# Normalised input for the last two products, and sums of squares by token without additions ahead of them

## The chip, the cores and the metric

The kernel runs on one core of a Trainium2 chip. The metric is the device time of one execution, in microseconds (us). The time before is given as the median of three runs; a further execution was taken with the hardware profiler, and all rows come from that one.

## The reference, cut to what matters

The kernel computes one block: a norm, a state-space mixer and a dilated attention side by side, an FFN with a causal convolution, a gated projection of a side input `p`, and a last norm. Only the end of it concerns the change:

```
h  = h + (gelu(gate) * (u2 @ ffn_w_up)) @ ffn_w_down
u3 = rms_norm(h, ple_norm_g)
h  = h + sigmoid(u3 @ ple_w_gate) * (p @ ple_w_proj)
return rms_norm(h, final_norm_g)
```

`x` is 512 tokens by 1024 features, all float32. `rms_norm(x, g)` is `x * rsqrt(mean(x*x) + 1e-6) * g`, with the mean over the features of a token.

## The kernel before, in words

**Layout.** Features lie on the 128 partitions and tokens along the free axis, so `h` is 8 tiles of 128 features by 512 tokens. A product `W.T @ u` for 128 output features runs over 8 blocks k of input features and leaves a 128x512 tile in PSUM.

**Three matmuls for one.** Each operand is split into a high part (rounded to the chip's fast float32 form, `F32R`) and a low part (the rest). `mm3` (lines 148 to 151) issues high by high, high by low and low by high. A weight chunk of 128x1024, the weights of one output tile, is loaded by DMA into `wr`, copied to `wh` by ScalarE (line 128) and subtracted to `wl` by VectorE (line 129); each has three buffers in turn. `u_split` (lines 158 to 160) makes the two parts of an input: the gain g of the norm is in there as a scale, the norm's factor by token is not.

**The factor comes in behind the product.** A factor by token can be taken out of the product, so the kernel computes `(h*g) @ W` first and multiplies the PSUM tile by `rb3` (the factor, spread over all partitions) afterwards. `rstd_full` (lines 235 to 253) makes `rb3` from the sum of squares `acc3`, beside the first products of this stage.

**The last stage (lines 998 to 1095).** The input `u3` has been split while the FFN's last products ran, and `pp` holds `p @ ple_w_proj`. The loop of lines 1031 to 1038 makes output tiles m = 0 to 5 over all 512 tokens: `gemm` into `eps`, then `ple(m)` (lines 1012 to 1025): VectorE multiplies PSUM by `rb3` (line 1014), ScalarE takes `tanh` (line 1023), two VectorE instructions (`stt`, recorded at line 422) fold in `pp` and update `h`. `sq_acc` squares the new `h` on ScalarE (line 204) and adds it to `acc4` on VectorE (line 205); `scale_g` (line 1028) writes `hg`, the new `h` times the last gain.

The tiles m = 6 and 7 are made twice, for two groups of 256 tokens (`LAST`, lines 1058 to 1080): m = 6 and 7 of the first group, then m = 6 and 7 of the second. The text calls these four products 6a, 7a, 6b and 7b; instructions of theirs have 256 columns. Their `ple` is the same but that in 7b the `tanh` (line 1017) writes a tile of its own and is followed by a tiny square root (line 1019), which makes the engine load the table for the square root early. The squares of 6a, 7a and 6b are added to `acc4` (line 1075); that of 7b is not.

**Sums and output.** `finish` (lines 1045 to 1055) sums over the features on TensorE: `stats` (lines 1006 to 1010) takes 128 tokens of a tile of squares as weights and a column of ones as the moving operand, one matmul for 128 tokens, run by the chip in two passes. For the first group one `stats` call on `acc4` is enough; it is put inside product 7b (`STATS_AT`, with an offset of -15 in the order). For the second group `stats` is called on `acc4` and on the squares of 7b. From the sums comes the last norm's factor by token, `y4`: with VectorE alone for the first group (`rstd_dve`), with a square root on ScalarE for the second (`rstd_of`). Then TensorE transposes `hg` to tokens on partitions (tile `fT`, line 1087), 4 transposes a tile, 8 tiles; ScalarE (line 1091) or VectorE (recorded at line 417) scales each by `y4` into `fo`, as the letters of `EVAC` say (A or D), and SyncE issues the store of 256 KB (line 1094).

**What sets the order.** Tiles of the pools have fixed numbers of buffers: 5 for `mm_tile` (PSUM, the products and half of the transposes), 4 for `t_tile` (the working tiles of `ple`, the squares). When the program is built, every engine gets its instructions in one fixed order, chosen by priority (the order of the program, moved ahead by `ahead(n)`: 300 for weights, `TAIL` = 40 for the end) among those that the builder's own clock thinks ready. On the chip each engine keeps that order, and an instruction that must wait holds up all behind it.

```
def mm3(ps, st, mv, first, last):
    PE.matmul(ps, st[0], mv[0], start=first, stop=False)
    PE.matmul(ps, st[0], mv[1], start=False, stop=False)
    PE.matmul(ps, st[1], mv[0], start=False, stop=last)
```

Of the kernel before, what the change touches and what calls it, by code (L numbers as in the profile page):

```python
# [10 lines left out]
F32R = mybir.dt.float32r  # L11
I32 = mybir.dt.int32
AF = mybir.ActivationFunctionType
ALU = mybir.AluOpType
# [5 lines left out]
KD = D // P  # L20
SEQ = 512
# [8 lines left out]
V_MIX, V_GB, V_GLUB, V_FFN, V_CW, V_CB, V_PLE, V_FIN, V_N = 0, 8, 24, 28, 36, 102, 124, 132, 140  # L30
# [9 lines left out]
WARM = 8  # L40
TAIL = 40
ST_AHEAD = -15
EVAC = "ADADADAD"
STATS_AT = (7, 0)
NLAST = 2
LAST = ((0, 1), (2, 3))
# [18 lines left out]
def tile_hybrid_block(ctx: ExitStack, tc: tile.TileContext, xT, xtok, pT, W, vecs, consts, ssm, out):  # L65
    nc = tc.nc
    ACT, DVE, POOL, PE = nc.scalar, nc.vector, nc.gpsimd, nc.tensor
# [8 lines left out]
    def slot(i, shape, name, dt=F32):  # L76
        return sb.tile([P] + shape, dt, tag=f"s{i}", name=name)
# [4 lines left out]
    def mm_tile(name):  # L82
        return pm.tile([P, 512], F32, tag="mm", name=name)

    def ax_tile(name):
        return px.tile([P, 512], F32, tag="ax", name=name)

    def t_tile(name):
        return ring.tile([P, 512], F32, tag="t", name=name, bufs=4)
# [12 lines left out]
    def v1(col):  # L102
        return vec[:, col:col + 1]
# [5 lines left out]
    def ahead(offset=AHEAD):  # L109
        return tc.high_priority(offset=offset)  # L110
# [37 lines left out]
# [5 lines that stand above are left out]
    def u_tiles(name):  # L153
        uh = [slot(f"uh{j}", [4, SEQ], f"{name}h{j}", F32R) for j in range(2)]
        ul = [slot(f"ul{j}", [4, SEQ], f"{name}l{j}", F32R) for j in range(2)]
        return ([uh[k // 4][:, k % 4, :] for k in range(KD)], [ul[k // 4][:, k % 4, :] for k in range(KD)])
# [42 lines left out]
    def sq_acc(acc, k, src):  # L199
        if k == 0:  # L200
            ACT.activation(acc, src, AF.Square)
        else:
            t = t_tile("sq")
            ACT.activation(t, src, AF.Square)
            DVE.tensor_tensor(acc, acc, t, op=ALU.add)
# [29 lines left out]
    def rstd_full(acc, name):  # L235
        hi = ring.tile([P, SEQ], F32R, tag="t", name=name + "_hi", bufs=4)
        lo = ring.tile([P, SEQ], F32R, tag="t", name=name + "_lo", bufs=4)
        ACT.activation(hi, acc, AF.Copy)
        DVE.tensor_tensor(lo, acc, hi.bitcast(F32), op=ALU.subtract)
        ps = ax_tile(name + "_ps")  # L240
        PE.matmul(ps, ones_r, hi, start=True, stop=False)
        PE.matmul(ps, ones_r, lo, start=False, stop=True)
        m = t_tile(name + "_m")
        DVE.tensor_scalar(m, ps, 1.0 / D, EPS, op0=ALU.mult, op1=ALU.add)
        t = t_tile(name + "_t")
        ACT.activation(t, m, AF.Sqrt)
        y = sb.tile([P, SEQ], F32, tag="acc", name=name + "_y")
        DVE.reciprocal(y, t)
        DVE.tensor_tensor(t, y, y, op=ALU.mult)
        DVE.tensor_tensor(t, t, m, op=ALU.mult)  # L250
        DVE.tensor_scalar(t, t, -0.5, 1.5, op0=ALU.mult, op1=ALU.add)
        DVE.tensor_tensor(y, y, t, op=ALU.mult)
        return y
# [151 lines left out]
    def gemm(ps, kt, mv):  # L405
        for k in range(kt):
            mm3(ps, wT.next(), (mv[0][k], mv[1][k]), k == 0, k == kt - 1)
# [4 lines left out]
    def tt(o, a, b, op):  # L412
        DVE.tensor_tensor(o, a, b, op=op)  # L413
# [7 lines left out]
    def stt(o, a, s, b, o0, o1):  # L421
        DVE.scalar_tensor_tensor(o, a, s, b, op0=o0, op1=o1)
# [445 lines left out]
    for m in range(2):  # L868
        ps = mm_tile("v0")
# [8 lines left out]
    for m in range(16):  # L878
        ps = mm_tile("gps")
# [10 lines left out]
    def split(hi, lo, src):  # L890
        ACT.activation(hi, src, AF.Copy)
        tt(lo, src, hi.bitcast(F32), ALU.subtract)
# [11 lines left out]
    for m in range(4):  # L904
        ps = mm_tile("lps")
        gemm(ps, 4, (parts(yh, 4), parts(yl, 4)))
        t = t_tile("lg")
# [8 lines left out]
    h = slot("x", [KD, SEQ], "h")  # L916
# [25 lines left out]
    for m in range(KD):  # L942
        ps = mm_tile("ops")
# [9 lines left out]
    u3 = None  # L953
    for part in range(2):
# [4 lines left out]
        for mi in range(HALF):  # L959
            m = part * HALF + mi  # L960
# [9 lines left out]
            t = t_tile("cv")  # L970
# [9 lines left out]
        if part == 1:  # L980
            u3 = u_tiles("u3")
            acc3 = sb.tile([P, SEQ], F32, tag="acc", name="acc3")
        for m in range(KD):
            ps = mm_tile("dps")
# [13 lines left out]
    for m in range(KD):  # L998
        ps = mm_tile("pps")
        gemm(ps, 2, (parts(ph, 2), parts(pl, 2)))  # L1000
        ACT.activation(pp[m // 4][:, m % 4, :], ps, AF.Copy)
    acc4 = slot("g1", [SEQ], "acc4")
# [3 lines left out]
    def stats(st, src, n, first, last):  # L1006

        for i in range(n):
            PE.matmul(st[:, i:i + 1], src[:, i * 128:(i + 1) * 128], ones[:, 0:1], start=first and i == 0, stop=last,
                      skip_group_check=True)  # L1010

    def ple(m, ps, c, last=False):
        t = t_tile("pg_")[:, c]
        tt(t, ps, rb3[:, c], ALU.mult)
        if last:
            th = t_tile("th")[:, c]
            ACT.activation(th, t, AF.Tanh, scale=0.5)

            ACT.activation(warm, th[:, 0:1], AF.Sqrt, bias=ones[:, 0:1], scale=0.0)
            stt(t, th, 1.0, pp[m // 4][:, m % 4, c], ALU.add, ALU.mult)  # L1020
            stt(h[:, m, c], t, 0.5, h[:, m, c], ALU.mult, ALU.add)
            return
        ACT.activation(t, t, AF.Tanh, scale=0.5)
        stt(t, t, 1.0, pp[m // 4][:, m % 4, c], ALU.add, ALU.mult)
        stt(h[:, m, c], t, 0.5, h[:, m, c], ALU.mult, ALU.add)

    def scale_g(m, c):
        ACT.activation(hg[m // 4][:, m % 4, c], h[:, m, c], AF.Copy, scale=v1(V_FIN + m))

    everything = slice(0, SEQ)  # L1030
    for m in range(KD - NLAST):
        ps = mm_tile("eps")
        gemm(ps, KD, u3)
        if m == 0:
            rb3 = rstd_full(acc3, "n3")
        ple(m, ps, everything)
        sq_acc(acc4, m, h[:, m, :])
        scale_g(m, everything)


    tail = range(KD - NLAST, KD)
    wl_ = [[wT.next() for k in range(KD)] for m in tail]
    y4 = []

    def finish(rs, c, sq, rstd):
        st = ax_tile("st4")
        if sq is None:
            with ahead(ST_AHEAD):
                stats(st, acc4[:, c], len(rs), True, True)
        else:  # L1050
            with ahead(TAIL):
                stats(st, acc4[:, c], len(rs), True, False)
                stats(st, sq, len(rs), False, True)
        with ahead(TAIL):
            y4.append(rstd(st[:, 0:len(rs)], f"n4_{rs[0]}", len(rs)))

    waiting = []
    for gi, rs in enumerate(LAST):
        c = slice(rs[0] * 128, rs[-1] * 128 + 128)
        end = gi == len(LAST) - 1  # L1060
        for m in tail:
            ps = mm_tile("eps")[:, 0:128 * len(rs)]
            for k in range(KD):
                if waiting and (m, k) == STATS_AT:
                    waiting.pop()()
                mm3(ps, wl_[m - tail[0]][k], (u3[0][k][:, c], u3[1][k][:, c]), k == 0, k == KD - 1)
            with ahead(TAIL):
                ple(m, ps, c, end and m == KD - 1)
                sq = t_tile("sq")[:, c]
                if m < KD - 1:  # L1070
                    ACT.activation(sq, h[:, m, c], AF.Square)
                else:
                    tt(sq, h[:, m, c], h[:, m, c], ALU.mult)
                if m < KD - 1 or not end:
                    tt(acc4[:, c], acc4[:, c], sq, ALU.add)
            scale_g(m, c)
        if end:
            finish(rs, c, sq, rstd_of)
        else:
            waiting.append(functools.partial(finish, rs, c, None, rstd_dve))  # L1080
    n = 0
    for rs, y in zip(LAST, y4):
        for j in range(2):
            for r in rs:
# [4 lines left out]
                yr = y[:, r - rs[0]:r - rs[0] + 1]  # L1089
                if EVAC[n] == "A":  # L1090
                    ACT.activation(o, pt, AF.Copy, scale=yr)
# [145 lines left out]
```

## Time and profile before

| | |
|---|---|
| median of 3 runs | 802.42 us (801.52 to 802.46) |
| the profiled execution, its own time | 801.21 us |
| its span (first to last instruction) | 799.4 us |
| busy: TensorE, VectorE, ScalarE | 99%, 62%, 43% of the span |
| the last stage's products (`eps`) | 743.16 to 788.3 us |
| stores of the output | first issued at 791.32 us, last at 795.7 us |

The page gives each engine's busy time and the chain of work that ended last: from the last instruction back, at each step to what released it. PE is TensorE, PEld its weight loads, DVE VectorE, ACT ScalarE, SP SyncE, whose queue issues the DMAs. A row of the timeline gives start, duration, engine, line, operation, the tile written and the tiles read, and in brackets how long the engine had been idle and who released it. Instructions overlap a little, so the step from one start to the next is shorter than a duration.

### The profile page before, as it was taken

The page shows a single profiled execution, that of the slowest core. Times are in us where ns is not written, and L with a number is a line of the kernel's source. Part 1 is how long each engine was busy: PE and PEld are TensorE (multiplying, and loading weights), DVE is VectorE, ACT ScalarE, POOL GpSimd, SP SyncE. Part 2 cuts the span into 40 slices and gives each one's busy share as a digit, 9 for nine tenths or more (in the row PEclk, how much of TensorE's full clock was granted, in tenths as well). Part 3 has the DMA queues.
Part 4 walks back from the last instruction along what each step waited for, and adds up shares of the span by engine and source line. Part 5 has one row for each costly group of instructions (what it writes and reads, how often), then busy time and mean ns, then how long its engine had stood idle before and what let it go on. Part 6 is the DMA issues. An engine that isn't in the chain of part 4 may idle for free.

```text
span 799.4 us, 10889 instructions
## 1 busy us (share of the span) xinstructions
PE 789.4 (99%) x4302; PEld 651.7 (82%) x4302; DVE 494.2 (62%) x960; ACT 346.0 (43%) x551; POOL 10.9 (1%) x10
## 2 busy tenths in 40 slices
PE   9999999999999999999999999999999999999996
PEld 7888888788777788888888888888888888888886
DVE  6974799933556558665865565333565565445586
ACT  6763634344444453344544343122344343335464
POOL 2001000000000000000000000000000000000000
PEclk9999999999999999999999999999999999999998
DMA  7721122231111223623323323323323322322302
GB/s 286 265 90 61 46 84 75 80 106 51 56 55 60 75 81 103 210 84 127 104 81 106 106 80 104 105 83 103 105 81 105 106 84 100 106 85 100 103 4 106
DMA packets 23811, 78.99 MB, mean 99 GB/s; under 512 B 2640, under 2 KB 3024, under 8 KB 23760
## 3 DMA queue, kind: packets, MB, share of 16 engines
q1 hardware_dynamic: 23616, 78.22, 29.0%
q8 instruction: 34, 0.56, 0.3%
q14 instruction: 17, 0.14, 0.1%
q10 hardware_dynamic: 144, 0.07, 0.0%
HBM read 76.18 MB, written 2.10 MB: 98 GB/s over the span
## 4 chain that ended last, share of the span: by engine, by line
PE 83%; DVE 10%; ACT 3%; issue 2%; DMA 1%; SPq 0%; DVEq 0%; ACTq 0%
PE dps L149 5%; PE pu L149 5%; PE pu L150 5%; PE pg L150 5%; PE pg L149 5%; PE dps L151 5%; PE dps L150 5%; PE pg L151 5%; PE pu L151 5%; PE gps L149 4%; PE gps L150 3%; PE gps L151 3%; PE pa L151 2%; PE pa L150 2%; DVE E L413 2%; PE pa L149 2%
## 5 line engine op out<-in xcount | busy, mean ns | idle before, releaser
L128 ACT ACTIVATE wh<-wr 128x1024 fp32r<-128x1024 f32 (+1 forms) x132 | 138.3, 1047 | 295.8 <-issue 66.3
L129 DVE TENSOR_TENSOR wl<-wr,wh 128x1024 fp32r<-128x1024 f32 (+1 forms) x132 | 159.2, 1206 | 69.9 <-ACT wh L128 69.4
L150 PE MATMUL pu<-u2l,wh 128*128 128x512 f32 x176 | 68.5, 389 | 0.0
L149 PE MATMUL pu<-u2h,wh 128*128 128x512 f32 x176 | 68.5, 389 | 0.0
L151 PE MATMUL pg<-u2h,wl 128*128 128x512 f32 x176 | 68.5, 389 | 0.0
L149 PE MATMUL pg<-u2h,wh 128*128 128x512 f32 x176 | 68.5, 389 | 0.0
L150 PE MATMUL pg<-u2l,wh 128*128 128x512 f32 x176 | 68.5, 389 | 0.0
L149 PE MATMUL dps<-ah,wh 128*128 128x512 f32 x176 | 68.5, 389 | 0.0
L150 PE MATMUL dps<-al,wh 128*128 128x512 f32 x176 | 68.5, 389 | 0.0
L151 PE MATMUL dps<-ah,wl 128*128 128x512 f32 x176 | 68.5, 389 | 0.0
L151 PE MATMUL pu<-u2h,wl 128*128 128x512 f32 x176 | 68.5, 389 | 0.0
L149 PE MATMUL pa<-wh,u1h 128*128 128x512 f32 x160 | 63.4, 398 | 0.0
L150 PE MATMUL pa<-wl,u1h 128*128 128x512 f32 x160 | 62.9, 393 | 0.0
L151 PE MATMUL pa<-wh,u1l 128*128 128x512 f32 x160 | 62.6, 393 | 0.1
L149 PE MATMUL gps<-u1h,wh 128*128 128x512 f32 x128 | 51.8, 404 | 0.0
L151 PE MATMUL gps<-u1h,wl 128*128 128x512 f32 x128 | 50.3, 393 | 0.0
L150 PE MATMUL gps<-u1l,wh 128*128 128x512 f32 x128 | 50.3, 393 | 0.0
L413 DVE TENSOR_TENSOR ext<-pg,n_y 128x512 f32<-128x512 f32 x22 | 15.2, 692 | 44.1 <-PE pg L151 44.1
L151 PEld LDWEIGHTS dps<-ah,wl 128*128 128x128 f32 x176 | 33.0, 188 | 6.9
L149 PEld LDWEIGHTS pu<-u2h,wh 128*128 128x128 f32 x176 | 33.0, 188 | 6.9
L151 PEld LDWEIGHTS pu<-u2h,wl 128*128 128x128 f32 x176 | 33.0, 188 | 6.9
L151 PEld LDWEIGHTS pg<-u2h,wl 128*128 128x128 f32 x176 | 33.0, 188 | 6.9
(305 smaller groups left out, 1499.6 us busy)
## 6 DMA issues: line engine op xcount, KB each, us to landing
wr<-in_W_dram SPq DMA_DIRECT2D x128, 512.0 KB, 3.2
xt<-in_xtok_dram SPq DMA_DIRECT2D x4, 512.0 KB, 8.0
h<-in_xT_dram SPq DMA_DIRECT2D x8, 256.0 KB, 4.8
out_dram<-fo SPq DMA_DIRECT2D x8, 256.0 KB, 2.3
x<-in_xT_dram SPq DMA_DIRECT2D x7, 256.0 KB, 5.4
wr<-in_W_dram SPq DMA_DIRECT2D x4, 256.0 KB, 5.3
cst<-in_consts_dram SPq DMA_DIRECT2D x1, 568.0 KB, 10.6
sp<-in_ssm_dram SPq DMA_DIRECT2D x1, 544.0 KB, 6.9
```

The lines of the kernel that those rows point to most:

```text
L128: ACT.activation(hi[:, c], raw[:, c], AF.Copy)
L129: DVE.tensor_tensor(lo[:, c], raw[:, c], hi[:, c].bitcast(F32), op=ALU.subtract)
L149: PE.matmul(ps, st[0], mv[0], start=first, stop=False)
L150: PE.matmul(ps, st[0], mv[1], start=False, stop=False)
L151: PE.matmul(ps, st[1], mv[0], start=False, stop=last)
L413: DVE.tensor_tensor(o, a, b, op=op)
```

## The change

The second group's inputs are made anew, with the norm's factor in them. As soon as `rb3` is there (behind product m = 0), `h * g * rb3` of the last 256 tokens is computed for all 8 feature blocks and split into two tiles `us`, which take the places of `ml` and `praw`. Products 6b and 7b read `us` in place of `u3`, so their PSUM needs no multiplication by `rb3`: `tanh` reads it directly. The squares of 6a, 7a and 6b are no longer added to `acc4`; `finish` gets the list of them and `stats` is called on `acc4` and on each. `EVAC` gives all four tiles of the first group to ScalarE.

```diff
-EVAC = "ADADADAD"
+EVAC = "AAAAADAD"
...
-    def ple(m, ps, c, last=False):
+    def ple(m, ps, c, scaled=False, last=False):
         t = t_tile("pg_")[:, c]
-        tt(t, ps, rb3[:, c], ALU.mult)
+        if not scaled:
+            tt(t, ps, rb3[:, c], ALU.mult)
         if last:
             th = t_tile("th")[:, c]
-            ACT.activation(th, t, AF.Tanh, scale=0.5)
+            ACT.activation(th, ps, AF.Tanh, scale=0.5)
...
-        ACT.activation(t, t, AF.Tanh, scale=0.5)
+        ACT.activation(t, ps if scaled else t, AF.Tanh, scale=0.5)
...
+    cl = slice(LAST[-1][0] * 128, SEQ)
     for m in range(KD - NLAST):
         ps = mm_tile("eps")
         gemm(ps, KD, u3)
         if m == 0:
             rb3 = rstd_full(acc3, "n3")
+
+            us = [slot(n, [KD, cl.stop - cl.start], f"us{j}", F32R) for j, n in enumerate(("qk2", "v"))]
+            for k in range(KD):
+                t = t_tile("us")[:, 0:cl.stop - cl.start]
+                stt(t, h[:, k, cl], v1(V_PLE + k), rb3[:, cl], ALU.mult, ALU.mult)
+                split(us[0][:, k, :], us[1][:, k, :], t)
         ple(m, ps, everything)
...
-    def finish(rs, c, sq, rstd):
+    def finish(rs, c, sqs, rstd, early):
         st = ax_tile("st4")
-        if sq is None:
-            with ahead(ST_AHEAD):
-                stats(st, acc4[:, c], len(rs), True, True)
-        else:
-            with ahead(TAIL):
-                stats(st, acc4[:, c], len(rs), True, False)
-                stats(st, sq, len(rs), False, True)
+        with ahead(ST_AHEAD if early else TAIL):
+            stats(st, acc4[:, c], len(rs), True, False)
+            for i, sq in enumerate(sqs):
+                stats(st, sq, len(rs), False, i == len(sqs) - 1)
...
-                mm3(ps, wl_[m - tail[0]][k], (u3[0][k][:, c], u3[1][k][:, c]), k == 0, k == KD - 1)
+                mv = (us[0][:, k, :], us[1][:, k, :]) if end else (u3[0][k][:, c], u3[1][k][:, c])
+                mm3(ps, wl_[m - tail[0]][k], mv, k == 0, k == KD - 1)
             with ahead(TAIL):
-                ple(m, ps, c, end and m == KD - 1)
-                sq = t_tile("sq")[:, c]
+                ple(m, ps, c, end, end and m == KD - 1)
+                sqs.append(t_tile("sq")[:, c])
                 if m < KD - 1:
-                    ACT.activation(sq, h[:, m, c], AF.Square)
+                    ACT.activation(sqs[-1], h[:, m, c], AF.Square)
                 else:
-                    tt(sq, h[:, m, c], h[:, m, c], ALU.mult)
-                if m < KD - 1 or not end:
-                    tt(acc4[:, c], acc4[:, c], sq, ALU.add)
+                    tt(sqs[-1], h[:, m, c], h[:, m, c], ALU.mult)
```

`split(hi, lo, src)` is a copy on ScalarE (line 891) and a subtraction on VectorE; `stt` and `tt` are one VectorE instruction each.

## Rows read from the trace of the kernel before

**Rows 1.** The page: busy time of each engine.

```profile
PE 789.4 (99%) x4302; PEld 651.7 (82%) x4302; DVE 494.2 (62%) x960; ACT 346.0 (43%) x551; POOL 10.9 (1%) x10
```

**Rows 2.** The chain that ended last, 785 to 799.4: start, us, what.

```profile
788.25 0.34 DVE acc L413
788.66 0.34 DVE pg__6376 L413
789.03 0.42 ACT th L1017
789.47 1.28 ACT L1019
790.76 0.30 ACT warm L1019
791.06 0.40 ACT hg L1028
791.46 1.15 ACT fo L1091 x2
793.61 0.75 DVE fo L417
```

**Rows 3.** Stretches: us, PE, PEld, DVE, ACT, POOL busy (x), clock, DMA share, GB/s.

```profile
758.87:765.00 6.13, 6.13 (x28) 5.07 (x28) 5.71 (x8) 3.35 (x5) 0.00 (x0) 1.00 0.12 48
765.00:772.96 7.96, 7.96 (x36) 6.57 (x35) 5.56 (x8) 5.46 (x8) 0.00 (x0) 1.00 0.01 2
772.96:782.40 9.44, 9.44 (x68) 8.89 (x67) 7.72 (x14) 4.85 (x9) 0.00 (x0) 1.00 0.00 0
```

**Rows 4.** Timeline of VectorE.

```profile
758.87 0.69 DVE L413 TENSOR_TENSOR pg__6011<-eps,n_y 128x512 f32<-128x512 f32 x1
...
785.40 0.43 DVE L413 TENSOR_TENSOR sq<-h 128x256 f32<-128x256 f32 x1
785.74 0.42 DVE L413 TENSOR_TENSOR pg__6323<-eps,n_y 128x256 f32<-128x256 f32 x1
786.07 0.42 DVE L413 TENSOR_TENSOR acc<-acc,sq 128x256 f32<-128x256 f32 x1
...
790.09 0.15 DVE L224 SCALAR_TENSOR_TENSOR n_y<-n_t,n_y 128x2 f32<-128x2 f32 x1
790.21 0.42 DVE L422 SCALAR_TENSOR_TENSOR h<-pg__6376,h 128x256 f32<-128x256 f32 x1
790.55 0.74 DVE L417 TENSOR_SCALAR fo<-fT,n_y 128x512 f32<-128x512 f32 x1
791.21 0.41 DVE L413 TENSOR_TENSOR sq<-h 128x256 f32<-128x256 f32 x1
```

**Rows 5.** Timeline of ScalarE.

```profile
765.28 1.06 ACT L128 ACTIVATE wh<-wr 128x1024 fp32r<-128x1024 f32 x1 [2.32 <-issue]
...
784.05 0.40 ACT L1023 ACTIVATE pg__6289<-pg__6289 128x256 f32<-128x256 f32 x1
```

**Rows 6.** Timeline of TensorE, products 7b and what follows.

```profile
784.77 0.28 PE L149 MATMUL eps<-u3h,wh 128*128 128x256 f32 x1
...
786.57 0.36 PE L1009 MATMUL st<-ones,acc 128*128 128x1 f32 x2
...
788.04 0.28 PE L151 MATMUL eps<-u3h,wl 128*128 128x256 f32 x1
788.16 0.60 PE L1087 MATMUL fT<-cst,hg 128*128 128x128 f32 x4
788.64 0.61 PE L1009 MATMUL st<-ones,acc 128*128 128x1 f32 x4
789.11 2.78 PE L1087 MATMUL fT<-cst,hg 128*128 128x128 f32 x22
```

**Rows 7.** Stretches at the end, columns as in rows 3.

```profile
792.00:792.50 0.50, 0.50 (x6) 0.48 (x6) 0.45 (x2) 0.50 (x2) 0.00 (x0) 1.00 0.61 238
...
795.00:795.50 0.50, 0.00 (x0) 0.00 (x0) 0.02 (x1) 0.00 (x0) 0.00 (x0) 0.72 0.66 246
795.50:796.00 0.50, 0.00 (x0) 0.00 (x0) 0.00 (x0) 0.00 (x0) 0.00 (x0) 0.50 1.03 381
```

**Rows 8.** The queue of SyncE, 788 to 800.

```profile
791.32 4.81 SPq L1094 DMA_DIRECT2D out_dram<-fo  x8
```

More of the change, by code (lines that the diff above doesn't have):

```diff
@@ L1060, in tile_hybrid_block @@
         end = gi == len(LAST) - 1
+        sqs = []
         for m in tail:
@@ L1065, in tile_hybrid_block @@
                     waiting.pop()()
-                mm3(ps, wl_[m - tail[0]][k], (u3[0][k][:, c], u3[1][k][:, c]), k == 0, k == KD - 1)
+                mv = (us[0][:, k, :], us[1][:, k, :]) if end else (u3[0][k][:, c], u3[1][k][:, c])
+                mm3(ps, wl_[m - tail[0]][k], mv, k == 0, k == KD - 1)
             with ahead(TAIL):
-                ple(m, ps, c, end and m == KD - 1)
-                sq = t_tile("sq")[:, c]
+                ple(m, ps, c, end, end and m == KD - 1)
+                sqs.append(t_tile("sq")[:, c])
                 if m < KD - 1:
-                    ACT.activation(sq, h[:, m, c], AF.Square)
+                    ACT.activation(sqs[-1], h[:, m, c], AF.Square)
                 else:
-                    tt(sq, h[:, m, c], h[:, m, c], ALU.mult)
-                if m < KD - 1 or not end:
-                    tt(acc4[:, c], acc4[:, c], sq, ALU.add)
+                    tt(sqs[-1], h[:, m, c], h[:, m, c], ALU.mult)
             scale_g(m, c)
         if end:
-            finish(rs, c, sq, rstd_of)
+            finish(rs, c, sqs, rstd_of, False)
         else:
-            waiting.append(functools.partial(finish, rs, c, None, rstd_dve))
+            waiting.append(functools.partial(finish, rs, c, sqs, rstd_dve, True))
     n = 0
```

## The prediction

> **What bounds the kernel now.** I read the page first: TensorE is busy 99% of the span [rows 1], so elsewhere only what lengthens or shortens TensorE's work counts. The chain of waits says where this stops: it leaves TensorE at about 770 us and runs over VectorE and ScalarE to the end, and through product 7b it runs over the addition of the squares of 6b, the multiplication by `rb3`, `tanh`, the table load, the tiny square root, `hg` and the output's scaling [rows 2]. So 1.3 us of table load and 0.3 us of square root stand on the path, and the change starts just in front of them. Third, the stretches of the last stage [rows 3] show how much room VectorE and ScalarE have for the new work; fourth, the timelines [rows 4 to 6] give prices and queue order; last, the stretches after 792 us [rows 7] show what the stores do. They keep the DMA engines full: the share is 0.61 in the first half microsecond, about 1.0 from then on but for one dip to 0.66 at 795.0, and it ends near 797.9. The span ends at 799.4. So from the first store on it is bandwidth that counts: 8 times 256 KB at some 385 GB/s are 5.45 us, and the dip is worth only 0.17 us.
>
> **The change part by part.** All sums are made against the profiled execution, 801.21 us with a span of 799.4. The four executions shown are 801.21, 801.52, 802.42 and 802.46, their mean 801.9; the profiled one lies 0.7 below that mean and 1.2 below the median.
>
> *The new input `us`.* It adds 8 multiplications, 8 copies and 8 subtractions of 256 columns, placed in the program ahead of `ple(0)`. On VectorE an instruction of this size lasts 0.42 but starts 0.34 after its neighbour (785.40, 785.74, 786.07) [rows 4]: 16 of them are 16 x 0.34 = 5.4 us, or 16 x 0.42 = 6.7 if they don't overlap. From `rb3` at 758.87 to 782.40 VectorE is busy 5.71 + 5.56 + 7.72 = 19.0 of 23.5 us [rows 3], so 4.5 are free, and 0.9 to 2.2 us run over. I take 0.9, since the 16 depend on each other only through ScalarE, and eight feature blocks can overlap. ScalarE gets 8 x 0.40 = 3.2 us [rows 5], against 23.5 - 13.7 = 9.8 free: nothing. TensorE wants `us` only at 781.9, behind 7a; that cover is some 15 us. What moves back is `ple(0)`, from 758.87 to about 766. It frees a PSUM buffer which the sixth product needs at about 770.7, so TensorE doesn't wait while this delay stays under 11 us.
>
> *The squares of the first group.* `sq` of 7a is done at 785.40 + 0.43 = 785.82. With 0.9 of overflow less the addition of 6a's squares (0.34) it is done at about 786.4. TensorE takes the sums at 786.57 [rows 6], so it is just in time.
>
> *The sums themselves.* For the first group there are three sources in place of one: 6 matmuls of two passes in place of 2, that is 8 passes more, and they stand inside 7b. What a pass costs there can be read: 7b takes 788.16 - 784.77 = 3.39 us, and 24 steps of 0.12 are 2.88, so the 4 passes of before cost 0.51, or 0.13 each. Behind the product 4 take 789.11 - 788.64 = 0.47, or 0.12 each [rows 6]. So 8 more cost 1.0 us; they cost nothing on this path if the queue puts them behind 7b. I take 1.0, because the place in the program, inside 7b, is unchanged: the last matmul ends at 789.3 in place of 788.32. The Trainium skill (TensorE: Matmul & The Clock Gate, "Wait — 56ns, not 53.3ns?") says that matmuls of few columns can follow each other every 25 ns or so; 8 passes would be 0.2 us by that and the sum below about 0.8 lower. The trace disagrees with 0.12 to 0.13; each pass here loads 128 columns of new weights, which by the same page's section "LDWEIGHTS (loading the stationary operand)" takes about 107 ns, and this the trace bears out.
>
> *`tanh` reads PSUM.* Before, 7b ended at 788.32, the multiplication started at 788.58 because VectorE was still adding, and `tanh` at 789.03 [rows 2, 4]. Now `tanh` follows TensorE alone: 789.3 and a few hundredths. That is 0.3 to 0.4 later than before, not earlier: the multiplication (0.34 on the chain) and the addition in front (0.34) go, and the passes take more than that back. The table load then ends near 791.1 and the tiny square root near 791.4.
>
> *The squares of 7b.* Before, a scaling of an output tile sat on VectorE ahead of them, 790.55 to 791.21 [rows 4]. It is gone, so they start right behind `h`: at 790.7 in place of 791.2, even with the later `tanh`. The second group's factor is then ready some 0.2 to 0.5 earlier.
>
> *The first group's scaling on ScalarE.* This pays for it. Before, VectorE did the first tile at 790.55, while ScalarE was still in its table load, and the first store went out at 791.32 [rows 4, 8]. Now the first tile must wait for ScalarE: 791.4 if it goes ahead of `hg`, 791.8 if behind it. With 0.62 for a tile (1.24 for two) it is done at 792.0 to 792.4, 0.7 to 1.1 later than before. From there ScalarE gives a tile every 0.62 us and the stores need 0.68, so bandwidth leads again, and the dip (0.17) closes since the second group's tiles come no later than they are wanted. Sum for the end: 0.7 to 1.1 less 0.2 to 0.3 for the dip and an easier start, **+0.6 us**. The end of the queue says +0.35: ScalarE's last tile is done at about 795.6, the last store issued near 796.05 in place of 795.7. I take +0.6, from the larger of the two conditions.
>
> **The rivals.**
>
> *A, the forecast (0.46):* +0.6, on the mean 802.5 us. No change that can be measured: about 0.2%, or 1.6 us, is what a measurement of this kernel can tell from none.
>
> *B, the passes are cheap or fall behind 7b (0.26).* Then `tanh` starts at 788.36, the load ends at 790.1, ScalarE is free at 790.4 and the first group's factor, ready at 790.24 before [rows 4], no longer waits: the first tile is done at 791.1, 0.2 earlier, and the dip closes: -0.4, 801.5 us. For it speaks that the queue's order is made by the builder's clock, which may think 7a's squares later; against it the rows of 0.13. The skill's 25 ns leads here too.
>
> *C, faster (0.10).* VectorE's removed work is all on the path (0.34 + 0.34 in front of `tanh`, 0.66 of the scaling, 0.26 of waiting at 788.32 to 788.58: 1.6) and the stores start as much earlier. That takes the first group's factor by 789, ahead of the table load; -1.7, 800.2 us. Against it: the factor of the first group hangs on 7a's squares, which come no sooner.
>
> *D, slower (0.18).* The place is ScalarE's queue at 763 to 766. There a weight copy waits 2.32 us for TensorE to let go of a buffer [rows 5]. If copies of `us` stand behind it, VectorE's subtractions wait with them, all four `t` buffers are taken, and VectorE stands still with its room used up. It decides from the point where 7a's squares come later than 786.6, of which only 0.2 us is left: from there each microsecond stops TensorE inside 7b by as much. Of the 2.32 about 2.1 at most arrive, 1.6 in the middle: +0.6 + 1.6 = +2.2, 804.1 us. For it speaks that VectorE is full on paper already; against it that the builder sees ScalarE busy too and may put the copies in front.
>
> **How the numbers follow.** A is the likeliest: 802.5 us. A and B are both inside 0.2%, 0.46 + 0.26 = 0.72; C gives 0.10 for faster, D 0.18 for slower. The range runs from 800.8 (between B and C; it leaves C out) to 804.2 (the middle of D; its upper half is left out), so 0.10 and 0.09 lie outside.
>
> **What would show it.** In the changed profile: 16 new VectorE instructions of 256 columns between 759 and 767, no wait of TensorE before 784; 12 passes of `st` inside 7b and its last matmul near 789.3; `tanh` of 7b released by TensorE within 0.1 us; the squares of 7b directly behind `h`; the first store issued at 792.0 to 792.4 and a DMA share of 1.0 without the dip. A first store before 791.2 makes A wrong in favour of B or C; a gap on TensorE in front of `st`, with VectorE idle near 765, makes it D. The forecast fails as well if the stores are not full from the first on.

## The result, and the profile after

The changed kernel takes 807.78 us, the median of 5 runs (807.19 to 808.61), beside 802.46 us for the kernel before in 5 runs (801.52 to 803.00). The ratio is 1.0071, with a 95% interval of 1.0059 to 1.0082: **slower by about 5.7 us** (0.0071 x 802.46; 4.7 to 6.6). The forecast was 802.5, with a range that ended at 804.2.

The profiled execution took 808.02 us, with a span of 806.2, so its span is 6.8 us above that of before. Not all of it is the change's: the last step of `rb3` starts at 759.09 here and at 758.14 before, behind identical code, and in the other profiles below it lies between 758.4 and 759.5. This leaves 6.8 - 0.95 = 5.85 us behind `rb3`.

Busy time of each engine, on the page of the changed kernel (beside [rows 1]):

```profile
PE 792.3 (98%) x4314; PEld 653.3 (81%) x4314; DVE 497.4 (62%) x969; ACT 349.7 (43%) x561; POOL 10.9 (1%) x10
```

VectorE works 3.2 us more than before (497.4 - 494.2). That is little, and its share of the span stays at 62%. A loss of 5.85 us can't be read from this row.

The chain that ended last, from 757 us to the end (start, us, what; compare [rows 2], which shows the end of that of before):

```profile
759.82 1.28 DVE us L422 x3
...
762.56 1.14 DVE wl L129
...
767.58 1.28 ACT L1024
...
779.65 0.70 DVE h L422
780.44 0.63 ACT sq L204
781.07 0.62 ACT hg L1029
781.69 0.53 ACT pg__6203 L1024
...
782.96 0.70 DVE h L422
```

Before, the chain left TensorE at about 770 us. Now it is already off TensorE when `us` starts on VectorE; it runs on over `ple(0)`, the load of the table for `tanh` (767.58) and then tile by tile: `h` on VectorE, squares, `hg` and `tanh` on ScalarE, `stt` and `h` on VectorE again. From 779.65 to 782.96 this circle takes 3.31 us.

Stretches of the changed kernel, columns as in [rows 3]:

```profile
759.82:766.82 7.00, 7.00 (x32) 5.79 (x32) 7.00 (x17) 4.37 (x10) 0.00 (x0) 1.00 0.12 47
766.82:786.97 20.15, 20.15 (x130) 18.36 (x129) 16.76 (x26) 12.18 (x19) 0.00 (x0) 1.00 0.01 1
```

In the first stretch, from `us` to the start of `ple(0)`, VectorE is busy without a gap: 17 instructions, the 16 of `us` and one subtraction of a weight chunk (1.14 us in the chain above), which in the kernel before stood behind the first steps of `ple`. In the second, from there to the end of `h` of tile 5, it is late by 7 us and yet stands still for 20.15 - 16.76 = 3.4 us.

The timeline of VectorE in the changed kernel (beside [rows 4]):

```profile
759.09 0.69 DVE L252 TENSOR_TENSOR n_y<-n_y,n_t 128x512 f32<-128x512 f32 x1
...
766.82 0.68 DVE L413 TENSOR_TENSOR pg__6045<-eps,n_y 128x512 f32<-128x512 f32 x1
...
773.09 1.23 DVE L129 TENSOR_TENSOR wl<-wr,wh 128x1024 fp32r<-128x1024 f32 x1 [1.05 <-ACT wh L128]
...
784.41 0.69 DVE L205 TENSOR_TENSOR acc<-acc,sq 128x512 f32<-128x512 f32 x1 [0.16 <-ACT sq L204]
785.55 0.69 DVE L422 SCALAR_TENSOR_TENSOR pg__6243<-pg__6243,pp 128x512 f32<-128x512 f32 x1 [0.44 <-ACT pg__6243 L1024]
786.28 0.69 DVE L422 SCALAR_TENSOR_TENSOR h<-pg__6243,h 128x512 f32<-128x512 f32 x1
...
791.38 0.42 DVE L413 TENSOR_TENSOR sq<-h 128x256 f32<-128x256 f32 x1
...
795.87 0.42 DVE L413 TENSOR_TENSOR sq<-h 128x256 f32<-128x256 f32 x1
796.21 0.15 DVE L224 SCALAR_TENSOR_TENSOR n_y<-n_t,n_y 128x2 f32<-128x2 f32 x1
```

`ple(0)` starts 7.0 us later than it could (759.82 to 766.82). The last `h` of the six full tiles, 786.28, is 27.19 us behind the last step of `rb3` (759.09). In the kernel before it stood 22.16 behind (780.30 - 758.14). Of that kernel, the end of product m = 0 on TensorE, the end of product m = 5, and VectorE:

```profile
748.21 0.39 PE L151 MATMUL eps<-u3h,wl 128*128 128x512 f32 x1
...
775.91 0.39 PE L151 MATMUL eps<-u3h,wl 128*128 128x512 f32 x1
```

```profile
766.38 1.23 DVE L129 TENSOR_TENSOR wl<-wr,wh 128x1024 fp32r<-128x1024 f32 x1 [1.63 <-ACT wh L128]
...
771.81 1.22 DVE L129 TENSOR_TENSOR wl<-wr,wh 128x1024 fp32r<-128x1024 f32 x1 [0.89 <-ACT wh L128]
...
776.99 0.69 DVE L422 SCALAR_TENSOR_TENSOR h<-pg__6169,h 128x512 f32<-128x512 f32 x1
...
778.43 0.69 DVE L205 TENSOR_TENSOR acc<-acc,sq 128x512 f32<-128x512 f32 x1 [0.16 <-ACT sq L204]
779.57 0.69 DVE L422 SCALAR_TENSOR_TENSOR pg__6209<-pg__6209,pp 128x512 f32<-128x512 f32 x1 [0.44 <-ACT pg__6209 L1023]
780.30 0.69 DVE L422 SCALAR_TENSOR_TENSOR h<-pg__6209,h 128x512 f32<-128x512 f32 x1
```

So 27.19 - 22.16 = **5.03 us of the 5.85 are already there at tile 5**. These rows of before also show the same circle with the same gaps, 0.16 and 0.44 us, and the same 3.31 us a tile (776.99 to 780.30). A product takes longer, 5.5 us (five of them lie between 748.21 and 775.91), so in the kernel before the circle was making good a late start of its own, that of `rb3`: the multiplication of tile 0 starts 10.3 us behind the end of its product (748.60 to 758.87), and only that of 7b, 0.26 us behind (788.32 to 788.58), has caught up. At 3.31 us a tile there is no time left for another 7 us. The squares of 7a then come at 791.38 in place of 785.40 [rows 4], which is 5.03 behind the offset of 0.95 again.

TensorE in product 7b and behind it (beside [rows 6]), and the first store (beside [rows 8]):

```profile
788.47 1.05 PE L1009 MATMUL st<-ones,acc 128*128 128x1 f32 x8 [0.67 <-DVE acc L205]
...
790.30 0.28 PE L151 MATMUL eps<-us,wl 128*128 128x256 f32 x1
...
792.46 0.50 PE L1009 MATMUL st<-ones,sq 128*128 128x1 f32 x4
...
798.38 4.48 SPq L1099 DMA_DIRECT2D out_dram<-fo  x8
```

7b ends 2.26 us later (790.30 against 788.04), 1.3 behind the offset. The passes for the squares of 7a (792.46) stand behind the product now, since the squares come that late. The first store is issued at 798.38 and the span ends 7.8 us behind it; before it was 791.32 and 8.08. This distance is 7.8 to 7.9 us in every one of the profiles below, so I read the end of each from its first store.

### The profile page after: what moved, and what is told of

Read it like the earlier page. It is cut to its first block, busy times and chain, and to the rows that moved or that the text cites. A ratio compares the mean times of both kernels' runs of the same rounds, so it can differ in the third digit from the quotient of the medians.

```text
span 806.2 us, 10935 instructions
## 1 busy us (share of the span) xinstructions
PE 792.3 (98%) x4314; PEld 653.3 (81%) x4314; DVE 497.4 (62%) x969; ACT 349.7 (43%) x561; POOL 10.9 (1%) x10
## 4 chain that ended last, share of the span: by engine, by line
PE 81%; DVE 12%; ACT 4%; issue 2%; DMA 1%; SPq 0%; ACTq 0%
PE dps L150 5%; PE pu L150 5%; PE pg L151 5%; PE pg L150 5%; PE pu L151 5%; PE dps L151 5%; PE dps L149 5%; PE pu L149 5%; PE pg L149 5%; PE gps L149 3%; PE gps L150 3%; PE gps L151 3%; PE pa L151 2%; PE pa L149 2%; PE pa L150 2%; DVE E L413 2%
## 5 line engine op out<-in xcount | busy, mean ns | idle before, releaser
L149 PEld LDWEIGHTS dps<-ah,wh 128*128 128x128 f32 x176 | 33.0, 188 | 6.9
L149 PEld LDWEIGHTS pg<-u2h,wh 128*128 128x128 f32 x176 | 33.0, 188 | 6.9
L150 PEld LDWEIGHTS pu<-u2l,wh 128*128 128x128 f32 x176 | 33.0, 188 | 6.9
## 6 DMA issues: line engine op xcount, KB each, us to landing
cst<-in_consts_dram SPq DMA_DIRECT2D x1, 568.0 KB, 10.3
```

## The experiments

Each lists its median, that of the kernel before beside it on the same chip, and the ratio with its 95% interval. The theories were that the loss is in making `us`, in reading it, in the passes inside 7b, or in the scaling on ScalarE; and, once it was found to be in making `us`, that it is paid as work on a full VectorE, or as a late start of `ple(0)`.

**The change without `us`.** `u3` and the multiplication stay; sums and `EVAC` are those of the change.

```diff
-            us = [slot(...)]
-            for k in range(KD): ...
...
-                mv = (us[0][:, k, :], us[1][:, k, :]) if end else (u3[0][k][:, c], u3[1][k][:, c])
+                mv = (u3[0][k][:, c], u3[1][k][:, c])
```

> The change without its new input: 6b and 7b read u3 and are multiplied by rb3 again; the sums by token without additions and the first group's scaling on ScalarE stay. Theory 1 (making the new input ahead of ple(0) puts VectorE some 5 us back, and the chain of the tiles never catches up): most of the loss is gone, 802 to 804 us, and h of m = 5 is done within 1 us of the kernel before. Theory 2 (the sums, their place in the queues and the scaling on ScalarE alone cost it): the loss stays, 806 to 808 us.

Measured: 804.45 beside 801.83, 1.0038 (1.0025 to 1.0051). Most of the loss goes with `us`, but some 2.6 us stay, a little above what was expected. `h` of tile 5 starts 22.15 behind the last step of `rb3` (780.84 - 758.69), as before.

**The kernel before with `us`, made and read.** Old sums, old `EVAC`.

```diff
+            us = [slot(...)]
+            for k in range(KD):
+                t = t_tile("us")[:, 0:cl.stop - cl.start]
+                stt(t, h[:, k, cl], v1(V_PLE + k), rb3[:, cl], ALU.mult, ALU.mult)
+                split(us[0][:, k, :], us[1][:, k, :], t)
...
+                mv = (us[0][:, k, :], us[1][:, k, :]) if end else (u3[0][k][:, c], u3[1][k][:, c])
```

> The kernel before with the new input alone: made behind rb3, read by 6b and 7b, no multiplication of their PSUM; the additions to acc4 and the old division of the scaling stay. Theory 1: 806 to 808 us. Theory 2: 801 to 803 us.

**The same, with `us` made but read by nothing**: the first five added lines alone.

> The kernel before, which also makes the new input but doesn't read it: 8 multiplications, 8 copies and 8 subtractions more, nothing else. Theory 1: as slow as with its use or slower, 806 to 809 us, since the two multiplications of PSUM stay. Theory 2, or a cost in reading the new input: 802 to 803 us.

**The change with the old `EVAC`.**

```diff
-EVAC = "AAAAADAD"
+EVAC = "ADADADAD"
```

> The change with the first group's scaling divided between ScalarE and VectorE as before. Theory 1: 0 to 1.5 us faster than the change, 806.3 to 807.8 us: the stores may start earlier, the chain ahead of them is the same. Theory 2: 2 us or more of the loss is gone, below 806 us.

Measured, all three beside 801.83: with `us` alone 808.87, 1.0086 (1.0070 to 1.0103); with `us` unread 808.89, 1.0089 (1.0074 to 1.0104); the change with the old `EVAC` 806.33, 1.0061 (1.0046 to 1.0076). Making `us` is the whole of its cost; what it saves in `ple` of 6b and 7b doesn't show. What the scaling on ScalarE costs isn't resolved here: 1.0061 and the change's 1.0071, some 0.8 us apart, lie within each other's intervals.

The pair of `us` alone and the change with the old `EVAC` differ by the sums only, and there the new sums *save* 2.5 us (808.87 - 806.33). In the kernel with `us` alone, VectorE's timeline and a stretch (columns as in [rows 3]) show where the time goes:

```profile
798.55 0.16 DVE L209 TENSOR_SCALAR n_m<-st 128x2 f32<-128x2 f32 x1 [2.05 <-PE st L1009]
798.62 0.15 DVE L224 SCALAR_TENSOR_TENSOR n_y<-n_t,n_y 128x2 f32<-128x2 f32 x1
```

```profile
796.00:798.00 2.00, 2.00 (x12) 2.00 (x10) 0.50 (x3) 0.98 (x3) 0.00 (x0) 0.50 0.00 0
```

In VectorE's order the second group's sums (798.55) stand ahead of the last step of the first group's factor (798.62), and wait 2.05 us for TensorE, whose granted clock is 0.50 there (1.2 GHz). In the changed kernel that last step runs at 796.21, ahead of the second group's sums. How much of the 2.5 us is this order and how much the clock isn't shown: the mean granted clock was 0.991 or 0.992 in all four executions with `us` alone, and 0.995 or 0.996 in three of the four with the new sums and the old `EVAC`.

**The new sums alone**, in the kernel before (the change without `us` and with the old `EVAC`).

```diff
+            stats(st, acc4[:, c], len(rs), True, False)
+            for i, sq in enumerate(sqs):
+                stats(st, sq, len(rs), False, i == len(sqs) - 1)
...
-                if m < KD - 1 or not end:
-                    tt(acc4[:, c], acc4[:, c], sq, ALU.add)
```

> The kernel before with the new sums alone: no additions of the squares of 6a, 7a and 6b, a stats call on each; the input and the division of the scaling as before. If the passes inside 7b carry the loss that is left without the new input: 803 to 804.5 us, with 7b's last matmul 1 us or more later than in the kernel before. If the scaling on ScalarE carries it: 801 to 802.5 us.

Measured: 803.85 beside 801.85, 1.0027 (1.0018 to 1.0036). TensorE in 7b:

```profile
787.12 0.73 PE L1009 MATMUL st<-ones,acc 128*128 128x1 f32 x6
...
790.30 0.28 PE L151 MATMUL eps<-u3h,wl 128*128 128x256 f32 x1
```

Counting all `st` rows from 787.12 to 790.10 there are 20 passes inside the product, where the kernel before has 4. The prediction counted 12: those of the first group. But the passes of the second group for `acc4` and for 6b, which wait for nothing of 7b, went in too.

**Eight more passes on zeros** in the kernel before, for their price by itself. The output is unchanged, since they add nothing.

```diff
-                stats(st, acc4[:, c], len(rs), True, True)
+                stats(st, acc4[:, c], len(rs), True, False)
+                stats(st, zero[:, 0:256], len(rs), False, False)
+                stats(st, zero[:, 0:256], len(rs), False, True)
```

> The kernel before with 8 more passes inside 7b: stats is called two times more on a tile of zeros, so the sums are the same. If a pass there costs 0.11 to 0.13 us of TensorE and 7b's end is on the path: 0.9 to 1.0 us slower, 802.7 to 803 us. If the passes hide, as TensorE waits anyway: within 0.3 us of the kernel before.

Measured: 802.99 beside 801.67, 1.0015 (1.0007 to 1.0024). TensorE, from the first pass in 7b to its last product:

```profile
786.84 0.36 PE L1009 MATMUL st<-ones,acc 128*128 128x1 f32 x2
...
789.32 0.38 PE L1091 MATMUL fT<-cst,hg 128*128 128x128 f32 x2
```

From 786.84 to 789.32 there are 12 passes and 9 products of 0.12 us: 2.48 - 1.08 = 1.40, or 0.12 a pass. Eight are 0.94 us of TensorE, and the time rises by 1.3 (0.6 to 1.9). The Trainium skill (TensorE: Matmul & The Clock Gate, "LDWEIGHTS (loading the stationary operand)") states that a load of weights takes their columns / 1.2 in ns; for 128 columns this is an estimate of 107 ns, and the 0.12 us of this trace bears it out.

**The change with the loop cut in two.** For m = 0 to 5 the multiplication and `tanh` of tile m are written ahead of both `stt`, the squares and `hg` of tile m - 1. Not an instruction more or less.

```diff
-        ple(m, ps, everything)
-        sq_acc(acc4, m, h[:, m, :])
-        scale_g(m, everything)
+        t = t_tile("pg_")
+        tt(t, ps, rb3, ALU.mult)
+        ACT.activation(t, t, AF.Tanh, scale=0.5)
+        if m:
+            back(m - 1, held)
+        held = t
+    back(KD - NLAST - 1, held)
```

`back(m, t)` is both `stt`, `sq_acc` and `scale_g` of tile m.

> The change, with the loop over m = 0 to 5 cut in two: multiplication by rb3 and tanh of tile m are put ahead of the two VectorE steps, the squares and hg of tile m - 1. Theory 1a (VectorE had room, but the strict alternation of one tile's steps between VectorE and ScalarE, 3.3 us a tile, kept it from catching up): a tile takes 2.6 to 2.8 us once VectorE is behind, so 805 to 806 us, 2 us or more below the change. Theory 1b (VectorE's work alone, 5.9 us, is too much): within 0.7 us of the change.

**The kernel before with the same cut.**

> The kernel before with the same cut of the loop and nothing else. Theory 1a: the chain from 772 us on is shorter, but TensorE's 7b ends where it did: 0.3 to 1.5 us faster, 800.5 to 801.7 us. Theory 1b: no difference, 801.5 to 802.5 us.

Measured beside 801.85: the change with the cut 804.49, 1.0034 (1.0021 to 1.0047); the kernel before with it 802.14, 1.0000 (0.9991 to 1.0010). VectorE in the change with the cut, and a stretch of it (columns as in [rows 3]):

```profile
776.87 0.68 DVE L422 SCALAR_TENSOR_TENSOR h<-pg__6157,h 128x512 f32<-128x512 f32 x1
...
779.27 0.68 DVE L422 SCALAR_TENSOR_TENSOR h<-pg__6197,h 128x512 f32<-128x512 f32 x1
...
780.59 0.69 DVE L422 SCALAR_TENSOR_TENSOR h<-pg__6237,h 128x512 f32<-128x512 f32 x1
```

```profile
776.87:779.27 2.40, 2.40 (x22) 2.40 (x22) 2.40 (x5) 1.88 (x4) 0.00 (x0) 1.00 0.00 0
```

VectorE has no waits here any more (busy 2.40 of 2.40), and a tile takes 2.40 us (776.87 to 779.27) in place of 3.31. `h` of tile 5 starts 22.12 behind the last step of `rb3` (780.59 - 758.47), where it stood in the kernel before (22.16). With the late start made good, the change costs what it costs without `us` (1.0038 and 1.0034). This is the run that decides between "5.4 us of work on a full engine" and "a start that comes too late for the circle to make it good": the work is still all there. In the kernel before the cut gains nothing, against what I had expected. Its VectorE:

```profile
777.10 0.69 DVE L413 TENSOR_TENSOR pg__6203<-eps,n_y 128x512 f32<-128x512 f32 x1 [1.37 <-PE eps L151]
```

With the cut it has caught up by tile 5 and waits for the product. `h` of tile 5 starts 20.38 behind `rb3` (779.28 - 758.90), so `us` still costs 1.7 us at this point in the cut loop (22.12 - 20.38). But TensorE's order has the first group's sums inside 7b, and they start 28.43 behind `rb3` with the cut and without it (787.33 - 758.90, 786.57 - 758.14): nothing that is done earlier shows in the time.

**`us` block by block**, block k just ahead of `ple(k)` (blocks 6 and 7 with 4 and 5).

```diff
-            for k in range(KD):
...
+        for k in ((0,), (1,), (2,), (3,), (4, 6), (5, 7))[m]:
```

> The change with the new input made a feature block at a time, each ahead of the ple of the same tile, in place of all eight ahead of ple(0). The same instructions. Theory 1a: the blocks fall into the gaps of the chain, 3 us or more below the change, 803 to 805 us. Theory 1b: within 1 us of the change, 806 to 808 us.

Measured: 806.81 beside 801.85, 1.0061 (1.0046 to 1.0076), a miss: the change's own 1.0071 is not told apart from it. In the profile 0.96 us came back by tile 5, whose `h` starts 26.23 behind `rb3` (784.69 - 758.46) in place of 27.19. VectorE, and the stretch of one tile (columns as in [rows 3]):

```profile
776.41 0.69 DVE L422 SCALAR_TENSOR_TENSOR h<-pg__6147,h 128x512 f32<-128x512 f32 x1
777.02 0.87 DVE L422 SCALAR_TENSOR_TENSOR us<-h,vec,n_y 128x256 f32<-128x256 f32 x2
...
780.52 0.69 DVE L422 SCALAR_TENSOR_TENSOR h<-pg__6195,h 128x512 f32<-128x512 f32 x1
```

```profile
776.41:780.52 4.11, 4.11 (x35) 4.07 (x35) 4.04 (x9) 2.49 (x5) 0.00 (x0) 1.00 0.00 0
```

The new instructions fill the gaps of the circle, but these are small, 0.60 us a tile; the rest lengthens it, to 4.11 us for this tile (776.41 to 780.52), which has two blocks in it and VectorE busy for 4.04. Here VectorE's own work is the limit.

**`us` and the cut, with the old sums and the old `EVAC`**: the kernel with `us` alone, and the loop cut as above.

> The kernel before with the new input made and read, and the loop over m = 0 to 5 cut in two as in the other run with that cut; the additions to acc4, the sums and the scaling as before. Theory 1a (the new input costs only what the chain can't take up, the rest of the loss is the sums and the scaling): 800.5 to 803 us, with 7b's tanh behind TensorE by less than 0.1 us. If the new input costs by itself (1b): 804 us or more, as with the cut and the new sums.

Measured: 802.11 beside 801.67, 1.0006 (0.9997 to 1.0015). The loss is gone; a gain isn't there. ScalarE, VectorE and the first store:

```profile
788.65 0.38 ACT L1018 ACTIVATE th<-eps 128x256 f32<-128x256 f32 x1
...
791.25 0.16 DVE L209 TENSOR_SCALAR n_m<-st 128x2 f32<-128x2 f32 x1 [0.44 <-PE st L1009]
791.33 0.15 DVE L224 SCALAR_TENSOR_TENSOR n_y<-n_t,n_y 128x2 f32<-128x2 f32 x1
...
792.28 4.48 SPq L1114 DMA_DIRECT2D out_dram<-fo  x8
```

`tanh` of 7b (788.65) comes earlier than before (789.03, [rows 2]), as the change means it to. But the last step of the first group's factor now stands behind the second group's sums (791.25) and starts at 791.33, where it was 790.09 [rows 4]: the first store waits for the second group.

**The same with the first group's factor moved ahead in the order** (and the second's moved back).

```diff
+FIRST, SECOND = 120, -20
...
-        with ahead(TAIL):
+        with ahead(SECOND if sq is not None else FIRST):
             y4.append(rstd(...))
```

> The version with the new input, the cut loop and the old sums, and in it the first group's factor put further ahead in the order and the second group's behind the first group's scaling on ScalarE. In all profiles so far the span ends 7.8 to 8.1 us after the first store. If the stores' bandwidth sets the end, a first store 0.4 to 0.7 us earlier than in that version gives 800.8 to 801.7 us, 0 to 0.8 us below the kernel before; if the second group's factor sets it, which now comes later: 802 us or more.

Measured: 802.21 beside 802.46, 1.0000 (0.9991 to 1.0009). The order that mattered stayed: VectorE takes the second group's `n_m` at 791.65 and the first group's last step at 791.73. So this didn't test what it was made for, and whether the earlier `tanh` can be turned into an earlier store is open.

**`us` off VectorE**: the gain by ScalarE, the factor and the subtraction on GpSimd; old sums, old `EVAC`, uncut loop.

```diff
-                stt(t, h[:, k, cl], v1(V_PLE + k), rb3[:, cl], ALU.mult, ALU.mult)
-                split(us[0][:, k, :], us[1][:, k, :], t)
+                ACT.activation(t, h[:, k, cl], AF.Copy, scale=v1(V_PLE + k))
+                POOL.tensor_tensor(t, t, rb3[:, cl], op=ALU.mult)
+                ACT.activation(us[0][:, k, :], t, AF.Copy)
+                POOL.tensor_tensor(us[1][:, k, :], t, us[0][:, k, :].bitcast(F32), op=ALU.subtract)
```

> The kernel before with the new input made without VectorE: the gain is multiplied in by ScalarE, the factor by GpSimd, the split is a copy on ScalarE and a subtraction on GpSimd; 6b and 7b read it, sums and scaling are as before. Theory 1 (VectorE's 5.9 us ahead of ple(0) are the loss): 800.5 to 803.5 us. If ScalarE's copies or the late table load are the loss: 805 us or more.

Measured: 812.69 beside 801.67, 1.0132 (1.0118 to 1.0145): far worse, where I had expected the loss to go. GpSimd and VectorE:

```profile
759.80 2.83 POOL L1043 TENSOR_TENSOR us<-us,n_y 128x256 f32<-128x256 f32 x4 [568.35 <-DVE n_y L252]
762.67 1.75 DVE L129 TENSOR_TENSOR wl<-wr,wh 128x1024 fp32r<-128x1024 f32 x1 [3.02 <-ACT wh L128]
769.23 0.69 DVE L413 TENSOR_TENSOR pg__6053<-eps,n_y 128x512 f32<-128x512 f32 x1 [4.81 <-POOL us L1045]
```

VectorE has nothing of `us` to do and stands still for 4.81 us: `ple(0)` needs one of the four `t` buffers, which the blocks of `us` hold until GpSimd has done with them. `ple(0)` starts at 769.23, even later than in the change. So here it isn't VectorE's work that counts, but how late `ple(0)` starts, whoever is the cause.

## Why the prediction was wrong

**The step that failed: "4.5 are free, and 0.9 to 2.2 us run over".** The size of the work was about right: the 16 instructions took 5.86 us (7.00 less the weight subtraction's 1.14), where the prediction had 5.4 to 6.7. Its "from 758.87 to about 766" agrees with the 7.0 measured, but its own sum gives 764.3 to 765.6; it had no term for the weight subtraction that now stands ahead of `ple(0)`. Wrong was that VectorE's 4.5 idle microseconds [rows 3] would take up work put in front of them. They are waits in VectorE's fixed order, of which its timeline names 4.1 us: 1.63 and 0.89 us for copies of weights, 0.42 once, and in each of two tiles the 0.16 and 0.44 us that VectorE waits for ScalarE, while ScalarE waits for VectorE in turn. Only the waits for weights shrank (one of 1.05 is left). A circle of two engines in a fixed order has its own period, 3.31 us before and after, and a delay that is there when it begins passes through to its end: of the 7.0 us, 5.02 are left at `h` of tile 4 (782.96 - 776.99, less the offset of 0.95) and 5.03 at tile 5. So 2.0 us were made good, where the prediction had 4.5. The change with the cut loop shows it: same work, no circle, the 5 us are back. The prediction saw that TensorE wouldn't wait for `ple(0)` and took this for the only one who could. From there "just in time" failed too: the squares of 7a were to be done by 786.4 and start at 791.38.

**The terms that were mis-sized or didn't come.** 8 passes at 0.13 us = 1.0: the price was right (0.12 by the spare passes), the number was not (16 more in 7b when the squares come in time, +2.0 us by the sums alone; 4 more in the changed kernel, where they come late). The parts don't add up: +7.0 for `us` and +2.0 for the sums, each alone, stand beside +5.7 for both and `EVAC`, since beside `us` the new sums save time (2.5 us, above).

**The scaling on ScalarE, "0.7 to 1.1 later".** The trace has this about right: from the first factor's end to the first store it is 2.02 us (796.36 to 798.38) in place of 1.08 (790.24 to 791.32), so 0.94. The profiles of the change without `us` and of the sums alone have `rb3` at 758.69 both, and the first store goes out at 794.78 with the scaling on ScalarE and at 793.78 without: 1.00. As a difference of times it isn't resolved: 0.6 us between the change without `us` (+2.6) and the sums alone (+2.0), with intervals that overlap.

**What held.** `tanh` of 7b follows TensorE directly where VectorE is in time (788.65, with `us` and the cut). The squares of 7b follow `h` (at 795.87, with nothing between them but two small steps of the factor). From the first store on the end is 7.8 to 7.9 us away in each changed profile, and the dip of [rows 7] (0.66) is closed, as predicted (the changed kernel, columns as there):

```profile
802.00:802.50 0.50, 0.00 (x0) 0.00 (x0) 0.00 (x0) 0.00 (x0) 0.00 (x0) 0.50 1.02 385
```

**The rivals.** D (slower, 0.18) had the sign and the sentence "VectorE is full on paper already", but not the mechanism: VectorE never stood still behind a weight copy in 759.82 to 766.82 (busy 7.00 of 7.00), and the time is 3.7 us above D's 804.1. The delay didn't go through TensorE either, which waited 0.67 us in 7b; it went by the squares and the sums straight into the first factor. B's cheap passes fell with the spare passes; that passes fall behind 7b came true for those of 6a and 7a, but because their squares were late, and it saved nothing. C's earlier `tanh` is real, but the store doesn't hang on it: it hangs on the first group's factor, which was the reason given against C.

**What stays open.** How much the load of the table for `tanh` (1.28 us, at 755.48 and off the chain before, at 767.58 and on it now) adds to the 5.03 wasn't tried by itself; in the change with the cut it stands in the same place (766.94) and the 5 us are gone, so by itself it doesn't keep the tiles late. Nor was `us` with buffers of its own, to be made in VectorE's gaps. No version here beats the kernel before: the best three, with the loop cut, are within 0.1% of it.

## What to carry to other kernels

Before idle time of an engine is taken as room, look at what ends its gaps, and at how late the chain already is: if it is another engine that waits for this one in turn, the period of the two is the limit, and of what delays the first round only that is made good which other waits take up (2.0 of 7.0 us here). Such a circle is broken by writing the next tile's first half ahead of this tile's second half; where the tiles then follow TensorE this gains nothing by itself, but it pays for work put in front. Count the passes that *may* start inside a product, not those that are meant to: whatever waits for nothing in it can be ordered into it.

## What the runs showed of the hardware that was not expected

TensorE's granted clock can fall inside the tail while TensorE is at work. Before, it was 1.00 as long as there were transposes, and 0.72 at 795.0 when TensorE had nothing left to do [rows 7]. In the change with the old `EVAC` TensorE waited 0.66 us in 7b, then worked on, and a stretch behind it (columns as in [rows 3]) reads:

```profile
792.00:794.00 2.00, 2.00 (x12) 2.00 (x11) 0.00 (x0) 0.00 (x0) 0.00 (x0) 0.50 0.00 0
```

TensorE's timeline there:

```profile
790.71 3.02 PE L1092 MATMUL fT<-cst,hg 128*128 128x128 f32 x13
```

At 0.50 (1.2 GHz; the two microseconds ahead of this stretch have a mean of 0.65) these 13 transposes take 3.02 us; 13 of the changed kernel (from 791.01, at 1.00, which is 2.4 GHz) take 1.62. VectorE stands still for 2.85 us, since the next sums come behind them. The changed kernel had waited as long in 7b (0.67 us) and kept 1.00 until 796, so a wait of this size doesn't always bring it, and what decides is open. The profiled execution is the slowest of four: it took 808.10 us at a mean clock of 0.992, the other three 806.13 to 806.35 at 0.995 or 0.996. So the fall seems to be no property of this kernel but of one execution in four, which widens the interval of the comparison with the change.

GpSimd needs 2.83 / 4 = 0.71 us for a multiplication of 128x256, against 0.42 on VectorE [rows 4]. Its subtractions (least, median and longest, in ns):

```profile
L1045 POOL TENSOR_TENSOR us<-us,us x8: 730/736/1727, 762.6 to 772.6; 128x256 fp32r<-128x256 f32 x8
```

A subtraction takes 0.74 as a rule, and one took 1.73. That one is among the first four (3.82 us from 762.59), beside which VectorE subtracts a weight chunk (762.67) in 1.75 us, 1.22 otherwise. That the two held each other up fits these rows, but wasn't tried by itself. That GpSimd had been idle for 568 us was no reason to put this work there.
